# Spreading the steps of the later modulation vectors over other stages, and reading the input back in sixteen pieces

## The chip, the cores and the metric

The kernel runs on one core of one Trainium2 chip. The metric is the device time of one execution in microseconds (us); the median of the runs counts.

## The reference, cut to what matters

One transformer block over 256 tokens of width 2048, with a context of 256 more tokens. A conditioning vector gives six modulation vectors; the block mixes a two-way recurrence and a windowed attention, and ends in a convolutional feed-forward part.

```python
mod_x = adaln(c, w_ada[l], b_ada[l])          # silu(c) @ w_ada + b_ada: 6 vectors of 2048
px = split_projection(modulate(x, norm1_g[l], mod_x[:, 0], mod_x[:, 1]) @ w_in[l])
rec_x, _, _ = hgrn2_bidirectional(px[0], px[1], px[2], px[3], px[4], lb, hgrn_norm_g[l], s_f, s_b)
att_x = windowed_attention(qx, kx, vx, kc, vc, attn_sink[l])
mix_x = gated_merge(rec_x, att_x, px[8], px[9], w_rec_proj[l], w_att_proj[l], w_out[l])
x_mid = x + mod_x[:, 2][:, None, :] * mix_x
ffn_x = conv_ffn(modulate(x_mid, norm2_g[l], mod_x[:, 3], mod_x[:, 4]), w_up[l], conv_w[l], conv_b[l], w_down[l])
new_x = x_mid + mod_x[:, 5][:, None, :] * ffn_x
```

The vectors 0 and 1 are needed at once. The vectors 2, 4, 3 and 5 (in the order of their use) are the "later modulation vectors" of this document: 2 is first needed in the output projection, 4 there too, 3 behind it, 5 in the down projection.

## The kernel before

**Weights.** All weights lie in one stream in HBM in the order of their use, in halves of 512 KB (eight tiles of 128x128, float32). `Stream.load` (L104 to L112) takes one half: SyncE issues the DMA into `raw` (four buffers), ScalarE rounds it into `whi` (L109), VectorE forms the rest `wlo` (L110); both have three buffers. TensorE multiplies with both parts. A load is put 60 instructions (`LEAD`) ahead of its use in the order by which the compiler places instructions. SyncE, VectorE and TensorE then each run their own list in that order: an instruction that waits holds all behind it on its engine.

**Stages**, in order of time in the trace (us): start and first projections to 149; the heads, 149 to 490; the attention's query projection to 548; the output gate of the recurrence with attention beside it to 615; the gates of the merge to 704, with the rest of the attention in it; the merge (sixteen column tiles, in eight pairs) to 889; the output projection (eight pairs, `mid_evac` behind each tile) to 985; up and down projections to the end.

**One head** `h` has two directions `d`. For each, `tform_all` (48 matmuls, two weight halves) makes the gate, and `hgrn_a` turns it into decays on ScalarE and VectorE. `hgrn_q` (L491) then prepares operands for `hgrn_b` (L506), the first small matmuls of the head, which TensorE has in its list in the next head, one `tform_all` later. Heads 4 and 6 are preceded by a `natural` projection, a long stretch of matmuls with little VectorE work.

**Steps.** `ada_steps` (L320) makes the later vectors: four vectors in two parts are eight blocks. A block is sixteen steps, each of which loads 512 KB of `w_ada` through GpSimd's DMA queue into `araw` (two buffers, L330) and adds it, scaled, into `acc` on VectorE (L333, L335); then two empty steps; then one that transposes `acc` on TensorE (L343) and reduces it (L344). `ada(n)` (L355) takes the next n of the 152 steps where it is called, 60 instructions (`LAG`) behind that place and behind the last `wlo` written so far. What the stages take is thus written out by hand as numbers in the calls of `ada`.

**The input.** `xm` (L761) takes the input again, to be added to the output projection's result. It has the place in memory (`qo`) of the recurrence's output, which is free once `y_rec` (L721, called in the gates) has read it. Two loads of 1 MB (L763), issued by SyncE; in the list of SyncE they stand where that place comes free.

Of the kernel before, what the change touches and what calls it, by code (L numbers as in the profile page):

```python
# [7 lines left out]
F32 = mybir.dt.float32  # L8
# [6 lines left out]
P = 128  # L15
T = 256
D = 2048
KT = D // P
# [32 lines left out]
def block_kernel(ctx, tc, xct, prm, cst, ada2, wst, out):  # L51
    nc = tc.nc
    V, S, PE = nc.vector, nc.scalar, nc.tensor

    cons = ctx.enter_context(tc.tile_pool(name="cons", bufs=1))
    big = ctx.enter_context(tc.tile_pool(name="big", bufs=1))
# [6 lines left out]
    def bank(pool=None):  # L63
        pool = pool or mm
        return pool.tile([P, 512], F32, name="bank" + ("m" if pool is mm else "s"))
# [20 lines left out]
    def par(n):  # L86
        o, w = POFF[n]
        return prm_t[:, o:o + w]
# [9 lines left out]
    class Stream:  # L98
# [20 lines left out]
        def next(self, n=1):  # L119
            if self.pos == 8:  # L120
                self.load()
            sl = slice(self.pos * P, (self.pos + n) * P)
            self.pos += n
            return self.hi[:, sl], self.lo[:, sl]
# [187 lines left out]
    qo = big.tile([P, 2, H, T], F32, name="qo", tag="qo")  # L312
# [42 lines left out]
    def ada(n=1):  # L355
        with tc.high_priority(offset=-LAG), tc.issue_after(st.last.ins):
            for _ in range(n):
                next(ada_it, None)
# [33 lines left out]
    def tform_all(o):  # L392
        for k in range(KT):
            mm3(o, *st.next(), hi_all(k), lo_all(k), k == 0, k == KT - 1)
            if k % 8 == 7:
                tick()

    def fold(dst, o):
        S.copy(dst, o[:, 0:T])
        V.tensor_tensor(dst, o[:, T:], dst, op=ALU.add)  # L400

    def natural(banks, tts):
        for i in range(8):
            ws = [st.next(4) for _ in range(2)]
            for b, tt in zip(banks, tts):
                for k2 in range(2):
                    kt = 2 * i + k2
                    mm3(b, *tok(kt, tt), *ws[k2], kt == 0, kt == KT - 1)
            tick()
# [81 lines left out]
    def hgrn_q(h):  # L491
        S.activation(QI, B_[:, :, 0:T], AF.Exp)
        for d in range(2):
            V.tensor_copy(dec[:, d, :], QI[:, d].rearrange("p (c t) -> p c t", t=CH)[:, :, LAST[d]])
        V.tensor_tensor(QI, QI, qo[:, 0, h, None, :].broadcast_to([P, 2, T]), op=ALU.mult)
        for d in range(2):
            c1, c2 = d, 1 - d
            q2 = QI[:, d].rearrange("p (a c t) -> p a c t", a=2, c=2)[:, :, c2, :]
            V.tensor_copy(QC[:, d], q2)
            V.tensor_tensor(q2, q2, dec4[:, d, :, c1, None].broadcast_to([P, 2, CH]), op=ALU.mult)  # L500
            kf = K_[:, d, d * P:d * P + P]
            V.tensor_scalar(K2[:, d, CH * c1:CH * c1 + CH], kf[:, CH * c1:CH * c1 + CH], dec4[:, d, d, c2:c2 + 1], None, op0=ALU.mult)
            V.tensor_copy(K2[:, d, CH * c2:CH * c2 + CH], kf[:, CH * c2:CH * c2 + CH])
            V.tensor_tensor(decb[:, d:d + 1], dec4[:, d, d, 0:1], dec4[:, d, d, 1:2], op=ALU.mult)
# [82 lines left out]
    def kv_evac(banks):  # L587
        kns = {}

        def norm(tt):  # L590
            S.copy(va[:, tt, :], banks[tt][:, 256:512])
            kn = scr.tile([P, 512], F32, name="t")
            headnorm(kn[:, 0:256], banks[tt][:, 0:256], 2, par("kg"))
            if tt < 2:
                rope(kn[:, 0:256], kn[:, 0:256], tt, 2, kn[:, 256:512])
            kns[tt] = kn

        def trans(tt):
            kn = kns.pop(tt)
            tp = bank(ms)  # L600
            for kv in range(2):
                PE.transpose(tp[:, kv * P:kv * P + P], kn[:, kv * P:kv * P + P], ident)
            S.copy(kT[:, :, tt * P:tt * P + P], tp[:, 0:256].rearrange("p (k e) -> p k e", k=2))

        def nxt(tt):
            trans(tt)
            if tt < 3:
                norm(tt + 1)
        norm(0)
        tasks.extend([lambda tt=tt: nxt(tt) for tt in range(4)])  # L610

    for h in range(H):
        if h == 4:
            bs = [bank() for _ in range(4)]
            natural(bs, range(4))
            ada(4)
            for tt in range(4):
                S.copy(vn[:, tt, 512:1024], bs[tt])
        if h == 6:
            bs = [bank() for _ in range(4)]  # L620
            natural(bs, range(4))
            ada(4)
            kv_evac(bs)
        for d in range(2):
            if 2 * h + d < 3:
                o = early_f[2 * h + d]
            else:
                o = bank()
                tform_all(o)
            hgrn_a(h, d, o)  # L630
            ada(0 if h > 5 else 2 if h else 1)
        hgrn_q(h)
        tasks += [lambda h=h: hgrn_e(h - 1), lambda h=h: hgrn_b(h), lambda h=h: hgrn_c(h), lambda h=h: hgrn_d(h)]
        ada(1)
        if h == 0:
            q_heads(4)
# [12 lines left out]
    for g in range(2):  # L649
        if g:  # L650
            bs = [bank() for _ in range(2)]
        natural(bs, range(2))
        ada(1)
        if not g:
            assert not tasks
            gr = big.tile([P, KT, T], F32, name="gr", tag="v")
            aq = gr[:, 0:H, :].rearrange("p (a c) t -> p a (c t)", a=2)
            PB = gr[:, H:, :].rearrange("p (h k) t -> p h (k t)", h=4)
        for tt in range(2):
            qn = aq[:, tt, g * 512:g * 512 + 512]  # L660
            headnorm(qn, bs[tt], 4, par("qg"))
            tmp = scr.tile([P, 512], F32, name="t")
            rope(qn, qn, tt, 4, tmp)

            def trans(g=g, tt=tt, qn=qn):
                tp = bank(ms)
                for i in range(4):
                    PE.transpose(tp[:, i * P:i * P + P], qn[:, i * P:i * P + P], ident)
                hs, ts = slice(4 * g, 4 * g + 4), slice(tt * P, tt * P + P)
                split(qTh[:, hs, ts], qTl[:, hs, ts], tp.rearrange("p (h e) -> p h e", h=4))  # L670
            tasks.append(trans)
# [44 lines left out]
    for h in range(0, H, 2):  # L716
        for i, o in enumerate(duo((xx, xx))):
            fold(qo[:, 0, h + i, :], o)
        ada(2)

    def y_rec(p):  # L721
        hs = slice(2 * p, 2 * p + 2)
# [4 lines left out]
    for j in range(0, KT, 2):  # L727
        for i, o in enumerate(duo((xx, xx))):
            fold(gr[:, j + i, :], o)
        if YR <= j < YR + 4:  # L730
            assert not tasks
            y_rec(j - YR)
            y_rec(j - YR + 1)
            ada(2)
        else:
            ada(2 + 2 * (j >= 8))
    for j in range(0, KT, 4):
        S.activation(gr[:, j:j + 4, :], gr[:, j:j + 4, :], AF.Sigmoid)

    assert not tasks, len(tasks)  # L740
    yb = big.tile([P, KT, 2, T], F32R, name="yb", tag="b")
    for j in range(0, KT, 2):
        gas = []
        for o in duo((xx, xx)):
            ga = scr.tile([P, 512], F32, name="t")
            fold(ga[:, 0:T], o)
            sig = S.activation(ga[:, 0:T], ga[:, 0:T], AF.Sigmoid)
            gas.append(ga)
        for i, ga in enumerate(gas):
            orec, oatt = duo((yre, yat), 8)  # L750
            fold(ga[:, T:], orec)
            V.tensor_tensor(gr[:, j + i, :], gr[:, j + i, :], ga[:, T:], op=ALU.mult)
            fold(ga[:, T:], oatt)
            V.tensor_tensor(ga[:, 0:T], ga[:, 0:T], ga[:, T:], op=ALU.mult)
            V.tensor_tensor(ga[:, 0:T], ga[:, 0:T], gr[:, j + i, :], op=ALU.add)
            split(yb[:, j + i, 1, :], yb[:, j + i, 0, :], ga[:, 0:T])
            ada(0 if j + i == 15 else 3 if i else 2)

    with tc.issue_after(sig.ins):
        S.preload_act_table_set("natural_log_exp_and_others")  # L760
    xm = big.tile([P, KT, T], F32, name="xm", tag="qo")  # L761
    for i in range(2):
        nc.sync.dma_start(xm[:, 8 * i:8 * i + 8, :], xct[:, 8 * i:8 * i + 8, 0:T])  # L763
    gate1, sc2, sh2, gate2 = [modv[:, i, :] for i in range(4)]
    ssa = scr.tile([P, 512], F32, name="rs", bufs=1)
    xa = big.tile([P, KT, T], F32, name="xa", tag="v")
# [19 lines left out]
    for j in range(0, KT, 2):  # L786
        for i, o in enumerate(duo((yb, yb))):
            with tc.high_priority(offset=RUSH if j == KT - 2 else 0):
                mid_evac(j + i, o)
        if 2 <= j < 8:  # L790
            ada(2 if j < 6 else 1)
        if j == 10:
            split(pre[:, 0, :, T:], pre[:, 1, :, T:], sh2[:, :, None].broadcast_to([P, KT, 2]))

# [229 lines left out]
```

## Time and profile before

| | us |
|---|---|
| median of three runs (1720.06 to 1724.96) | 1720.73 |
| the profiled execution's own time | 1723.61 |
| its span, first to last instruction | 1721.8 |
| TensorE busy in the span | 1692.8 |
| VectorE busy | 1203.1 |
| ScalarE busy | 837.4 |

The difference between own time and span lies before the first and behind the last instruction. TensorE's share (98%) is an average: where it is idle has to be read stage by stage, and the same holds for VectorE's 70%.

### The profile page before, as it was taken

The numbers are of one execution on the slowest core, as the hardware profiler recorded it, in microseconds if no ns is written. First come the engines' busy times: TensorE is split into PE (matmuls) and PEld (weight loads), VectorE is DVE, ScalarE is ACT, GpSimd is POOL, SyncE is SP. The second block draws the span as 40 slices with busy tenths as digits, with TensorE's granted clock in tenths as the row PEclk, the third lists the DMA queues.
The fourth block names the chain that finished last, engine by engine and source line by source line (L and its number), as shares of the span: only waits on it lengthen the run. The fifth ranks groups of instructions, "written<-read, shape, count | busy, mean of one in ns | idle before, by whom it ended". The sixth has DMA issues, their size and how long they took to land.

```text
span 1721.8 us, 24746 instructions
## 1 busy us (share of the span) xinstructions
PE 1692.8 (98%) x9438; PEld 1430.6 (83%) x9438; DVE 1203.1 (70%) x1890; ACT 837.4 (49%) x1278; POOL 69.0 (4%) x132
## 2 busy tenths in 40 slices
PE   6999999999999999999999999999999999999999
PEld 2668888888888887888888998888888888888887
DVE  4438876565669887788878797777766655666565
ACT  4237443342555665455554565555555434554332
POOL 0000100100000001010100000000000000000000
PEclk9999999999999999999999999999999999999999
DMA  9986724624345658787877567777655555555564
GB/s 375 379 331 223 258 98 158 196 80 153 111 135 192 212 185 292 265 288 246 310 242 231 190 223 259 231 249 252 232 183 185 194 184 195 184 194 186 190 201 148
DMA packets 104008, 371.84 MB, mean 216 GB/s; under 512 B 11344, under 2 KB 13776, under 8 KB 103888
## 3 DMA queue, kind: packets, MB, share of 16 engines
q1 hardware_dynamic: 85456, 303.14, 51.1%
q0 software_dynamic: 18432, 67.12, 12.1%
q8 instruction: 74, 1.21, 0.3%
q14 instruction: 46, 0.38, 0.1%
HBM read 368.11 MB, written 2.10 MB: 215 GB/s over the span
## 4 chain that ended last, share of the span: by engine, by line
PE 85%; DMA 6%; DVE 5%; issue 3%; ACT 1%; SPq 0%; POOL 0%; DVEq 0%; POOLq 0%; ACTq 0%
PE bankm L68 77%; PE banks L68 5%; DMA araw<-in_ada_dram 5%; DVE wlo L110 1%; DVE acc L335 1%; DMA ringq<-in_wst_dram 1%; ACT whi L109 1%; DVE xraw L230 0%; PE banks L343 0%; PE banks L524 0%; PE banks L532 0%; PE banks L698 0%; SPq L116 0%; ACT t L220 0%; PE banks L533 0%
## 5 line engine op out<-in xcount | busy, mean ns | idle before, releaser
L68 PE MATMUL bankm<-hl,whi 128*128 128x512 f32 (+1 forms) x3392 | 1055.1, 392 | 0.7 <-DVE t L400 0.7
L110 DVE TENSOR_TENSOR wlo<-raw,whi 128x1024 fp32r<-128x1024 f32 x498 | 606.0, 1219 | 301.4 <-ACT whi L109 299.9
L109 ACT CAST whi<-raw 128x1024 fp32r<-128x1024 f32 x498 | 520.4, 1046 | 555.6 <-PE bankm L68 481.2
L68 PEld LDWEIGHTS bankm<-hl,wlo 128*128 128x128 f32 x3104 | 582.8, 188 | 140.7 <-DVE wlo L110 9.5
L68 PE MATMUL bankm<-hl,wlo 128*128 128x256 f32 (+2 forms) x3104 | 665.1, 287 | 6.6 <-DVE wlo L110 6.4
L68 PEld LDWEIGHTS bankm<-hl,whi 128*128 128x128 f32 x3392 | 534.7, 189 | 21.1 <-DVE t L400 1.0
L335 DVE SCALAR_TENSOR_TENSOR acc<-araw,csil,acc 128x1024 f32<-128x1024 f32 x120 | 153.7, 1281 | 36.4 <-DMA araw<-in_ada_dram 35.7
L68 PE MATMUL bankm<-whi,hl 128*128 128x512 f32 x512 | 166.6, 398 | 3.3 <-ACT hl L206 2.6
L68 PEld LDWEIGHTS bankm<-whi,hl 128*128 128x128 f32 x512 | 96.7, 189 | 25.4 <-ACT hl L206 4.4
L330 POOL DMA_DIRECT2D araw<-in_ada_dram x128 | 68.8, 537 | 1153.8 <-DVE acc L335 664.5
L68 PE MATMUL bankm<-wlo,hl 128*128 128x512 f32 x256 | 100.5, 393 | 0.0
L68 PE MATMUL bankm<-yb,whi 128*128 128x512 f32 x256 | 80.8, 397 | 0.0
L68 PE MATMUL bankm<-g,whi 128*128 128x512 f32 x256 | 80.4, 395 | 0.0
L68 PEld LDWEIGHTS bankm<-g,wlo 128*128 128x128 f32 x256 | 48.1, 188 | 11.4
L68 PEld LDWEIGHTS bankm<-yb,wlo 128*128 128x128 f32 x256 | 48.1, 188 | 11.3
L68 PEld LDWEIGHTS bankm<-wlo,hl 128*128 128x128 f32 x256 | 48.5, 190 | 9.6
L849 DVE SCALAR_TENSOR_TENSOR xm<-bankm,modv,xm 128x256 f32<-128x256 f32 x96 | 42.2, 480 | 18.4 <-PE bankm L68 18.3
L831 ACT ACTIVATE fs<-fs,prm 128x256 f32<-128x256 f32 x44 | 26.5, 602 | 55.9 <-DVE fs L400 55.9
L68 PE MATMUL bankm<-yb,wlo 128*128 128x256 f32 x256 | 50.6, 279 | 0.0
L68 PE MATMUL bankm<-g,wlo 128*128 128x256 f32 x256 | 50.3, 278 | 0.0
L195 DVE TENSOR_REDUCE tn<-banks 128x8 f32<-128x32 f32 x8 | 1.5, 191 | 65.9 <-ACT whi L109 51.4
L832 DVE SCALAR_TENSOR_TENSOR fs<-fs,prm,fs 128x255 f32<-128x255 f32 x44 | 21.3, 484 | 26.7 <-ACT fs L831 26.7
(214 smaller groups left out, 1242.1 us busy)
## 6 DMA issues: line engine op xcount, KB each, us to landing
raw<-in_wst_dram SPq DMA_DIRECT2D x490, 512.0 KB, 4.0
araw<-in_ada_dram POOLq DMA_DIRECT2D x128, 512.0 KB, 4.7
ringv<-in_wst_dram SPq DMA_DIRECT2D x24, 512.0 KB, 8.7
ringq<-in_wst_dram SPq DMA_DIRECT2D x20, 512.0 KB, 9.6
araw<-in_wst_dram SPq DMA_DIRECT2D x10, 512.0 KB, 8.8
xraw<-in_xct_dram SPq DMA_DIRECT2D x8, 512.0 KB, 10.2
raw<-in_wst_dram SPq DMA_DIRECT2D x8, 384.0 KB, 8.4
ringkT<-in_wst_dram SPq DMA_DIRECT2D x5, 512.0 KB, 10.2
```

What stands on the lines that cost most here:

```text
L68: return PE.matmul(o, l, r, start=start, stop=stop, skip_group_check=True)
L109: S.copy(hi, raw)
L110: self.last = V.tensor_tensor(lo, raw, hi.bitcast(F32), op=ALU.subtract)
L195: V.tensor_reduce(m8, aps.rearrange("p (q g c) -> p q c g", q=4, g=4)[:, :, 0:2, :], axis=AX.X, op=ALU.add)
L330: nc.gpsimd.dma_start(raw, ada2[idx])
L335: V.scalar_tensor_tensor(acc, raw, csil[:, kt, 0:1], acc, op0=ALU.mult, op1=ALU.add)
L831: S.activation(t, s, AF.Identity, bias=cb[:, f:f + 1], scale=cw[:, f, 1:2])
L832: V.scalar_tensor_tensor(t[:, 1:T], s[:, 0:T - 1], cw[:, f, 0:1], t[:, 1:T], op0=ALU.mult, op1=ALU.add)
L849: V.scalar_tensor_tensor(xm[:, j, :], o[:, T * i:T * i + T], gate2[:, j:j + 1], xm[:, j, :], op0=ALU.mult, op1=ALU.add)
```

## The change

The number of steps that each stage takes is set anew; the steps themselves and their order stay. By the calls, the stages took and take:

| stage | steps before | steps after |
|---|---|---|
| heads | 46 | 68 |
| query projection | 2 | 4 |
| output gate | 8 | 12 |
| gates | 20 | 16 |
| merge | 37 | 16 |
| output projection | 5 | 8 |
| up projection | 34 | 28 |

The two loads of `xm` behind the merge become sixteen of 128 KB in it, one for each column tile. Each is held back by a copy of one column into the place that it will write (VectorE, 128x1), which itself reads the tile's `ga` after its second fold.

```diff
         if h == 4:
             natural(bs, range(4))
-            ada(4)
+            ada(6)
...
         if h == 6:
             natural(bs, range(4))
-            ada(4)
+            ada(6)
...
             hgrn_a(h, d, o)
-            ada(0 if h > 5 else 2 if h else 1)
+            ada(2 if h > 5 else 3 if h else 1)
...
         natural(bs, range(2))
-        ada(1)
+        ada(2)
...
     for h in range(0, H, 2):
         for i, o in enumerate(duo((xx, xx))):
             fold(qo[:, 0, h + i, :], o)
-        ada(2)
+        ada(3)
...
         else:
-            ada(2 + 2 * (j >= 8))
+            ada(2)
...
+    xm = big.tile([P, KT, T], F32, name="xm", tag="qo")
     for j in range(0, KT, 2):
...
             fold(ga[:, T:], oatt)
+
+            V.tensor_copy(xm[:, j + i, 0:1], ga[:, T:T + 1])
+            nc.sync.dma_start(xm[:, j + i, :], xct[:, j + i, 0:T])
             V.tensor_tensor(ga[:, 0:T], ga[:, 0:T], ga[:, T:], op=ALU.mult)
...
-            ada(0 if j + i == 15 else 3 if i else 2)
+            ada(1)
...
-    xm = big.tile([P, KT, T], F32, name="xm", tag="qo")
-    for i in range(2):
-        nc.sync.dma_start(xm[:, 8 * i:8 * i + 8, :], xct[:, 8 * i:8 * i + 8, 0:T])
...
-        if 2 <= j < 8:
-            ada(2 if j < 6 else 1)
+        if 2 <= j < 10:
+            ada(2)
```

## Rows read from the trace of the kernel before

**Rows 1.** The page, busy time, share of the span and instructions of each engine.

```profile
PE 1692.8 (98%) x9438; PEld 1430.6 (83%) x9438; DVE 1203.1 (70%) x1890; ACT 837.4 (49%) x1278; POOL 69.0 (4%) x132
```

**Rows 2.** By stage: stretch; length; PE, PEld, DVE, ACT, POOL busy; clock; DMA; GB/s.

```profile
149.00:490.00 341.00, 336.63 (x1723) 283.58 (x1722) 233.98 (x449) 152.46 (x266) 23.19 (x42) 0.99 0.47 156
...
548.00:615.00 67.00, 67.00 (x385) 58.17 (x384) 55.02 (x100) 46.96 (x79) 3.18 (x6) 1.00 0.59 193
615.00:704.00 89.00, 84.95 (x484) 72.73 (x483) 70.03 (x102) 48.71 (x75) 8.48 (x16) 1.00 0.77 266
704.00:889.00 185.00, 182.59 (x1052) 158.50 (x1051) 154.71 (x212) 93.52 (x145) 16.96 (x32) 1.00 0.80 274
889.00:985.00 96.00, 96.00 (x573) 84.58 (x571) 77.05 (x129) 47.63 (x72) 2.12 (x4) 1.00 0.63 205
```

**Rows 3.** Waits of TensorE from 140 us on: waiter, releaser, total, times, longest.

```profile
PE bankm L68 <- DVE wlo L110: 6.4, 5, 3.1
```

**Rows 4.** Timeline, late gates, one engine after another: start, length, operation [idle before].

```profile
679.70 0.50 PE L68 MATMUL bankm<-hl,wlo 128*128 128x256 f32 x2 [0.76 <-DVE wlo L110]
688.65 0.50 PE L68 MATMUL bankm<-hl,wlo 128*128 128x256 f32 x2 [3.10 <-DVE wlo L110]
...
686.18 1.28 DVE L335 SCALAR_TENSOR_TENSOR acc<-araw,csil,acc 128x1024 f32<-128x1024 f32 x1 [3.47 <-DMA araw<-in_ada_dram]
...
665.84 0.39 SPq L763 DMA_DIRECT2D xm<-in_xct_dram  x1
...
671.80 0.68 SPq L763 DMA_DIRECT2D xm<-in_xct_dram  x1
```

**Rows 5.** Late gates: busy time (as rows 2), and a DMA issue (KB each, us to landing).

```profile
682.00:693.00 11.00, 7.91 (x46) 6.58 (x45) 7.53 (x9) 4.00 (x4) 1.59 (x3) 1.00 0.85 327
...
xm<-in_xct_dram SPq DMA_DIRECT2D x2, 1024.0 KB, 10.4
```

**Rows 6.** Instructions on `araw`: durations in ns, least, median, most.

```profile
L335 DVE SCALAR_TENSOR_TENSOR acc<-araw,csil,acc x120: 1267/1281/1289, 157.3 to 1232.1; 128x1024 f32<-128x1024 f32 x120
...
L329 DVE COPY araw<-prm x2: 144/146/147, 148.4 to 148.4; 128x1 f32<-128x1 f32 x2
```

**Rows 7.** Head 1: timeline of ScalarE, VectorE, TensorE; busy time (as rows 2) behind it.

```profile
210.33 0.63 ACT L466 ACTIVATE hb<-hb 128x512 f32<-128x512 f32 x1
...
216.15 0.54 DVE L467 TENSOR_SCALAR hb<-hb,lb_t 128x512 f32<-128x512 f32 x1
...
221.67 1.18 PE L68 MATMUL banks<-hb 128*64 128x64 f32 x8 [1.78 <-DVE hb L499]
...
223.00:225.00 2.00, 1.98 (x8) 1.75 (x9) 2.00 (x9) 1.34 (x3) 0.00 (x0) 0.50 0.00 0
```

**Rows 8.** Head 3, second direction: timeline of VectorE and TensorE.

```profile
277.15 1.29 DVE L335 SCALAR_TENSOR_TENSOR acc<-araw,csil,acc 128x1024 f32<-128x1024 f32 x1 [1.17 <-DMA araw<-in_ada_dram]
...
283.77 0.19 DVE L503 COPY hb<-hb 128x64 f32<-128x64 f32 x1
...
284.17 3.35 PE L68 MATMUL banks<-hb 128*128 128x128 f32 x24
```

**Rows 9.** Heads 4 and 5: `hgrn_a` of their second directions on VectorE; busy time (as rows 2).

```profile
348.72 0.55 DVE L467 TENSOR_SCALAR hb<-hb,lb_t 128x512 f32<-128x512 f32 x1 [0.69 <-ACT hb L466]
...
376.43 0.55 DVE L467 TENSOR_SCALAR hb<-hb,lb_t 128x512 f32<-128x512 f32 x1 [0.82 <-ACT hb L466]
...
338.90:386.00 47.10, 47.10 (x237) 39.58 (x237) 33.85 (x84) 24.33 (x45) 0.74 (x1) 1.00 0.26 87
```

**Rows 10.** Output projection, busy time (as rows 2) of a stretch with steps and one without.

```profile
923.00:934.00 11.00, 11.00 (x65) 9.62 (x64) 10.81 (x18) 4.91 (x9) 1.06 (x2) 1.00 0.73 230
...
956.00:967.00 11.00, 11.00 (x65) 9.63 (x64) 8.45 (x15) 5.67 (x9) 0.00 (x0) 1.00 0.59 194
```

**Rows 11.** The end: a wait of SyncE's queue, and small DMA issues (as rows 3, 5).

```profile
SPq L862 <- DVE xm L849: 11.0, 2, 8.0
...
out_dram<-xm SPq DMA_DIRECT2D x2, 128.0 KB, 1.8
```

## Prediction

> **What bounds the kernel now.** Read the busy times first: TensorE works 1692.8 of 1721.8 us [rows 1]. The 29 us that are left are all that a change of this kind can give, and most of them lie in the start, which it doesn't touch. So the next view is the busy time by stage, where the reader looks for stages in which TensorE's column is shorter than the stage: 4.37 us are missing in the heads, none in the output gate, 4.05 in the gates, 2.41 in the merge, none in the output projection [rows 2]. The waits say who ended the pauses: from 140 us on, five waits for `wlo`, 6.4 us, are the largest entry [rows 3]. By the timeline four of these five lie in gates and merge, and the two largest, 0.76 and 3.10 us, are in the late gates [rows 4].
>
> There two things meet. The two 1 MB loads of `xm` are issued at 665.84 and 671.80 us [rows 4], as soon as their place is free and not where the code has them; they take 10.4 us to land, and even behind them the DMA share is 0.85 at 327 GB/s [rows 5], where gates and merge together have 0.77 and 0.80 [rows 2]. In the same pairs the kernel takes four steps instead of two, so VectorE comes to additions whose data is still under way: one waits 3.47 us, and the `wlo` behind it in VectorE's list lets TensorE wait 3.10 us [rows 4]. In the merge VectorE is busy 154.71 of 185 us [rows 2] and the pauses are of the same kind, only shorter.
>
> The heads' missing time is another matter. [...]
>
> **The change part by part.** *Steps leave gates and merge.* An addition takes 1.28 us on VectorE [rows 6]. Counting which of the moved steps are additions (a block has sixteen, then two empty steps, then the transposition), the gates lose three of sixteen, the merge nineteen of 32. The merge's VectorE falls from 154.7 by 19 x 1.28 = 24.3 us to 130.4 of 182.6 us. In the gates the groups of four are gone. I take all 4.05 + 2.41 = 6.46 us as gained: in the output gate and the output projection VectorE is as busy (82% and 80%) and TensorE has no pause [rows 2]. The lower bound of the gain is what the two largest waits name, 3.86 us [rows 4].
>
> *The sixteen loads.* They move the same 2 MB in the merge, over 185 us instead of some 16. The nearest rows for one are the 128 KB stores at the end, 1.8 us to landing, and the 1 MB loads, 10.4 us [rows 5, 11]; 16 x 1.8 = 29 us of flight in 185 us, beside other transfers: nothing on the path. Each tile's load is wanted by `mid_evac` in the next stage, so it is early by a stage. The sixteen copies cost VectorE 16 x 0.145 = 2.3 us [rows 6], covered by the 24.3 us that leave; without that cover they would cost at most that. The new wait is SyncE's: it waits for the copy, and behind it stand the weight loads. The end of the kernel shows such a wait, 8.0 us long, with weight loads behind it [rows 11], and no `wlo` wait falls there. I take 0; the other end is a rival below.
>
> [...]
>
> *Steps enter the heads.* Nineteen more additions, 24.3 us, and one more transposition, whose matmuls are only moved. Over the stage that fits: VectorE has 234 of 341 us [rows 2]. Head by head it doesn't quite. A head lasts 376.43 - 348.72 = 27.7 us; without additions VectorE is busy 33.85 of 47.1 us, so 19.9 us per head [rows 9]; seven additions make 28.9 us, 1.2 more than there is. Heads 2 to 5 are of that kind; what is over can fall into the two `natural` stretches behind heads 3 and 5. What counts is VectorE's work from the end of `tform_all` to `hgrn_b`. In head 3 an addition already lies in it, with 1.17 us of waiting for its data; VectorE ends at 283.96, TensorE comes at 284.17 without a pause [rows 8]. So 0.2 us of slack are left there with one addition of 2.5 us, some 2.7 without. Seven steps in a head put one or two there. The bounds: below, the 5.35 us of head 1 are given back (-5.35); above, two more heads like head 1 (+10.7). I take half of the 1.2 us in each of four heads, **+2.0 us**, nearer to head 3, which is as dense (two steps 3.4 us apart) and pauses nowhere.
>
> *Steps enter output gate and output projection.* Three more additions and a transposition make 55.0 + 3.8 + 1.5 of 67 us, 90%; I take 0. In the output projection a pair without steps uses 8.45 of 11 us of VectorE; two additions make 11.0 of 11 in four pairs running. One stretch with 10.81 is there, with no pause [rows 10]. Bounds 0 and four pauses like 0.76 [rows 4], 3.0; I take **+0.5**. The up projection loses six steps and had no pause: 0.
>
> The sum: -6.46 + 2.0 + 0.5 = **-4.0 us**. The profiled execution took 1723.61 us, 2.9 above the median of 1720.73; it becomes 1719.6, and the median 1716.7.
>
> **The rivals.** *The heads take everything without a pause* (head 3 speaks for it, the 28.9 of 27.7 us against): -6.46, 1714.3. *The pause of head 1 goes as well*: -11.8, 1708.9; the steps of heads 0 and 1 change little (block one has only sixteen additions, and all came before head 1's `hgrn_a`), so it is unlikely.
>
> *Slower: heads that pause as head 1 does.* The mechanism: VectorE's list is fixed, an addition that waits for its DMA holds `hgrn_a` and `hgrn_q`, TensorE reaches `hgrn_b` first, pauses, and loses half its clock. Price 5.35 us per head. From 6.46 / 5.35 = 1.2 heads on it eats the gain: two heads give 1725.0, three 1730.3. For it: head 1, and a slack of 0.2 us. Against: in the heads the DMA share is 0.47, in the merge 0.80 [rows 2], so data lands sooner.
>
> [...]
>
> *Slower: SyncE's queue.* If a wait for the copy holds the weight loads longer than the buffers last, each tile may pause. At 1 us for each of sixteen tiles, it is +16: 1730.3 together with the gain. It decides from waits as long as the 8.0 us of the end [rows 11], if they come with all buffers empty.
>
> *The stalls only move* (to output gate and output projection): 1720.7.
>
> **How the numbers follow.** Forecast 1716.7: 0.45, its own range 1713.5 to 1720. Heads without pause 0.20; head 1 cured too 0.08; heads with clock loss 0.14, half of it two heads, half three or more; the queue 0.05; moved only 0.08. A measurement of this kernel tells about 0.3% from no change, 5.2 us: faster means under 1715.6, slower over 1725.9. Faster: 0.20 + 0.08 + 0.09 of the forecast's own = 0.37. Slower: 0.07 + 0.05 = 0.12. The rest, 0.51, is the same. The range reaches from 1708, for the cured head 1, to 1727, for two heads with clock loss; it leaves out three such heads and the queue, 0.12.
>
> **What would show it.** Right: `xm` issues spread through the merge, no 1 MB issue near 666 us, gates and merge with TensorE busy throughout, VectorE at some 73% of the merge; in the heads waits of the small matmuls for `hb` of some 2 us in all beside head 1's. Wrong: waits for `wlo` still in gates or merge (then it was not the burst); clock under 1.00 in heads 2 to 7; SyncE waits on the copy with `whi` late behind it.

## The result, and the profile after

| | before | after |
|---|---|---|
| median (20 runs each), us | 1723.3 | 1728.93 |
| lowest to highest, us | 1718.79 to 1731.86 | 1721.5 to 1738.97 |
| profiled execution, own time, us | 1723.61 | 1725.86 |
| its span, us, and its mean granted clock | 1721.8, 0.997 | 1723.8, 0.994 |

The ratio of after to before is 1.0033, its 95% interval 1.0018 to 1.0047: slower by some 0.3%, where 0.2% faster was forecast. The median of before lies 2.6 us above that of the three runs of the prediction.

First the busy time by stage (stretch; length; PE, PEld, DVE, ACT, POOL busy; clock; DMA share; GB/s), to be laid beside [rows 2].

```profile
149.00:490.00 341.00, 330.86 (x1677) 278.71 (x1676) 243.47 (x445) 144.64 (x252) 32.58 (x60) 0.98 0.55 180
...
548.00:615.00 67.00, 66.15 (x383) 57.15 (x382) 62.65 (x110) 45.44 (x75) 5.61 (x11) 1.00 0.66 213
615.00:704.00 89.00, 88.90 (x513) 77.23 (x512) 64.32 (x104) 52.94 (x86) 3.36 (x7) 1.00 0.59 196
704.00:889.00 185.00, 185.00 (x1066) 161.48 (x1065) 141.76 (x205) 93.90 (x146) 9.49 (x18) 1.00 0.74 246
889.00:985.00 96.00, 96.00 (x564) 84.25 (x563) 81.53 (x134) 48.83 (x73) 4.22 (x8) 1.00 0.69 239
```

The stretches are the same times in both traces, while the changed kernel lags by 10.5 us at the last head and 2.9 us at the output projection (below), so its rows hold slightly earlier work. Gates and merge now miss 0.10 us of TensorE together, where they missed 4.05 and 2.41. The heads miss 10.14 us instead of 4.37, at a clock of 0.98 instead of 0.99. The waits of TensorE from 140 us on (waiter, releaser, total, times, longest) say who ended the pauses:

```profile
PE banks L68 <- DVE hb L499: 8.6, 6, 3.1
PE banks L68 <- DVE hb L536: 1.0, 1, 1.0
...
PE bankm L68 <- DVE wlo L110: 0.8, 1, 0.8
```

The `wlo` waits of [rows 3] are all but gone, and in their place stands the first operand of `hgrn_b` (L499), which is the pause that head 1 had in [rows 7]. TensorE's timeline has the larger ones in heads 4 and 6 (start, length, operation, in brackets the idle time before it and what ended it):

```profile
220.81 1.18 PE L68 MATMUL banks<-hb 128*64 128x64 f32 x8 [1.52 <-DVE hb L499]
...
283.67 2.87 PE L68 MATMUL banks<-hb 128*64 128x64 f32 x20 [0.97 <-DVE hb L499]
...
359.83 4.76 PE L68 MATMUL banks<-hb 128*64 128x64 f32 x20 [2.30 <-DVE hb L499]
...
470.56 3.42 PE L68 MATMUL banks<-hb 128*64 128x64 f32 x20 [3.07 <-DVE hb L499]
```

How the wait comes about is read from VectorE's timeline in head 4, second direction:

```profile
350.06 1.28 DVE L335 SCALAR_TENSOR_TENSOR acc<-araw,csil,acc 128x1024 f32<-128x1024 f32 x1 [2.12 <-DMA araw<-in_ada_dram]
351.26 0.54 DVE L467 TENSOR_SCALAR hb<-hb,lb_t 128x512 f32<-128x512 f32 x1
...
352.74 1.28 DVE L335 SCALAR_TENSOR_TENSOR acc<-araw,csil,acc 128x1024 f32<-128x1024 f32 x1 [0.47 <-DMA araw<-in_ada_dram]
...
356.65 1.28 DVE L335 SCALAR_TENSOR_TENSOR acc<-araw,csil,acc 128x1024 f32<-128x1024 f32 x1
...
359.55 0.23 DVE L499 COPY hb<-hb 128x128 f32<-128x128 f32 x1
```

One addition stands ahead of `hgrn_a` and two between it and `hgrn_b`'s operand. Two of the three find their data not yet landed, and VectorE stands still for 2.12 + 0.47 = 2.59 us, which is a little more than TensorE's pause of 2.30. The additions themselves take 3.8 us there, so that this row alone leaves open which of the two is too much; the experiments below separate them. Head 6 has the same picture: 1.34 + 1.55 = 2.89 us of waiting for data in two additions, 3.07 us of pause:

```profile
461.09 1.28 DVE L335 SCALAR_TENSOR_TENSOR acc<-araw,csil,acc 128x1024 f32<-128x1024 f32 x1 [1.34 <-DMA araw<-in_ada_dram]
...
464.27 1.29 DVE L335 SCALAR_TENSOR_TENSOR acc<-araw,csil,acc 128x1024 f32<-128x1024 f32 x1 [1.55 <-DMA araw<-in_ada_dram]
```

Behind these two pauses the granted clock is down to 0.50. Busy time in short stretches around head 4's pause, and behind head 6's (columns as above, the clock third from the end):

```profile
358.00:360.00 2.00, 0.17 (x2) 0.17 (x2) 2.00 (x8) 1.71 (x3) 0.53 (x1) 0.99 0.36 49
360.00:362.00 2.00, 2.00 (x10) 1.65 (x10) 2.00 (x7) 0.00 (x0) 0.00 (x0) 0.50 0.56 221
...
366.00:368.00 2.00, 2.00 (x9) 1.59 (x8) 1.31 (x3) 1.01 (x2) 0.00 (x0) 0.80 0.22 47
...
474.00:476.00 2.00, 2.00 (x8) 1.90 (x9) 1.90 (x2) 0.99 (x3) 0.00 (x0) 0.50 0.88 297
```

From 360 to some 367 us TensorE has 0.50 (0.52 in the mean of these 7 us), which costs 3.4 us.

**Where the time went.** The same instruction in both traces gives the lead or lag at its place. The `hgrn_a` of the second direction of heads 4 and 5 stood at 348.72 and 376.43 [rows 9]; after, at 351.26 (above) and at

```profile
383.07 0.54 DVE L467 TENSOR_SCALAR hb<-hb,lb_t 128x512 f32<-128x512 f32 x1
```

so the lag is 2.5 us and then 6.6; the 28 us between them hold head 4's pause and its half clock. Read on like this, the changed kernel is 0.9 us ahead at the first head (start differs by that), 10.5 behind at the last one (491.20 against 480.69), 2.9 behind at the first `mid_evac`, and 2.0 at the end. The heads cost 11.4 us, and the way to the output projection gives back 7.6. The 11.4 are made up so: the pauses from 149 to 500 us sum to 10.58 us against 4.24, so 6.3 more; half clock behind heads 1, 4 and 6 (granted in the mean: 0.81 from 221 to 230 us, 0.52 from 360 to 367, 0.82 from 470 to 474 and 0.50 to 476) costs 1.7 + 3.4 + 1.7 = 6.8 us against 3.4 before (0.52 from 223 to 230), so 3.4 more; the remaining 1.7 us were not read by themselves, but are about the size of the third transposition (eight matmuls of 0.27 us), which now lies in the heads and no longer behind them.

**One profile is not the median.** Of the 20 executions after, the fastest (1721.5) had a mean granted clock of 0.997, the slowest (1738.97) 0.990. The span times what is missing of the clock, 5.2 and 17.4 us, makes up 12.2 of the 17.5 us between them. The median of that product is 11.2 us over the 20 runs after, and 5.2 us over 29 runs of before, taken on another chip for the experiments. This difference of 6.0 us is as large as that of the medians, 5.6. The clock is on record to three decimals, so each product is good to 0.9 us only. By this estimate the pauses gained in gates and merge and those lost in the heads came out even, and the lost clock makes the kernel slower.

### The profile page after: what moved, and what is told of

It is laid out like the page before. It is cut to its first block, busy times and chain, and to the rows that moved or that the text cites. A ratio compares the mean times of both kernels' runs of the same rounds, so it can differ in the third digit from the quotient of the medians.

```text
span 1723.8 us, 24762 instructions
## 1 busy us (share of the span) xinstructions
PE 1695.1 (98%) x9438; PEld 1433.9 (83%) x9438; DVE 1204.6 (70%) x1906; ACT 835.4 (48%) x1278; POOL 68.9 (4%) x132
## 4 chain that ended last, share of the span: by engine, by line
PE 75%; issue 11%; DMA 7%; DVE 5%; ACT 1%; SPq 0%; POOL 0%; POOLq 0%; DVEq 0%; ACTq 0%
PE bankm L68 70%; DMA araw<-in_ada_dram 6%; PE banks L68 4%; DVE acc L335 1%; DVE wlo L110 1%; DMA ringq<-in_wst_dram 1%; DVE xraw L230 0%; PE banks L343 0%; PE banks L698 0%; DVE hb L473 0%; DVE hb L474 0%; DVE hb L489 0%; PE banks L524 0%; SPq L116 0%; ACT t L220 0%
## 5 line engine op out<-in xcount | busy, mean ns | idle before, releaser
L68 PEld LDWEIGHTS bankm<-yb,wlo 128*128 128x128 f32 x256 | 48.1, 188 | 11.4
L68 PEld LDWEIGHTS bankm<-g,wlo 128*128 128x128 f32 x256 | 48.1, 188 | 11.4
L68 PE MATMUL banks<-hb 128*128 128x128 f32 (+2 forms) x256 | 39.3, 285 | 9.8 <-DVE hb L499 8.6
L68 PEld LDWEIGHTS banks<-hb 128*128 128x128 f32 (+1 forms) x256 | 33.6, 187 | 16.1 <-DVE hb L499 9.7
```

The source lines that it names most:

```text
L68: return PE.matmul(o, l, r, start=start, stop=stop, skip_group_check=True)
```

## The experiments

Three theories stood at the start. Theory A: gates and merge gain what was forecast, and the heads' added steps take more than that, by pauses and clock. Theory B: the sixteen loads with their copies cost something. Theory C: VectorE is short of time wherever the steps are put. Each ratio is to the kernel before on the same chip: its median was 1723.81 us for the first four kernels below (29 runs), 1724.91 for the next four (29 runs) and 1724.68 for the last (14 runs).

**The sixteen loads alone**, on the kernel before, its steps untouched:

```diff
+    xm = big.tile([P, KT, T], F32, name="xm", tag="qo")
     for j in range(0, KT, 2):
...
+            V.tensor_copy(xm[:, j + i, 0:1], ga[:, T:T + 1])
+            nc.sync.dma_start(xm[:, j + i, :], xct[:, j + i, 0:T])
...
-    xm = big.tile([P, KT, T], F32, name="xm", tag="qo")
-    for i in range(2):
-        nc.sync.dma_start(xm[:, 8 * i:8 * i + 8, :], xct[:, 8 * i:8 * i + 8, 0:T])
```

> The kernel before with the sixteen loads of xm alone; all steps stay where they were. Theory A (the steps in the heads made the kernel slower, the loads are innocent): the two pauses of the late gates (0.76 and 3.10 us) go, heads as before, so 1 to 5 us faster than before (ratio 0.997 to 1.000). Theory B (the loads hold SyncE's queue or VectorE in the merge): slower than before by some 5 us (ratio about 1.003), with raw loads late in the merge.

Measured: 1722.01 us (12 runs), ratio 0.9982 (0.9969 to 0.9994). In time the loads cost nothing and seem to bring a little. In the late gates one pause is left where [rows 4] have 0.76 and 3.10 us; the merge on the other hand misses 5.42 us instead of 2.41, in a profiled execution that was the slowest of the twelve (1726.51 us). Timeline of TensorE and busy time by stage of this kernel:

```profile
686.48 0.50 PE L68 MATMUL bankm<-hl,wlo 128*128 128x256 f32 x2 [1.41 <-DVE wlo L110]
```

```profile
704.00:889.00 185.00, 179.58 (x1021) 155.38 (x1020) 152.37 (x221) 90.90 (x142) 16.89 (x32) 0.99 0.82 279
```

**The steps alone**, the two 1 MB loads as before:

```diff
-            V.tensor_copy(xm[:, j + i, 0:1], ga[:, T:T + 1])
-            nc.sync.dma_start(xm[:, j + i, :], xct[:, j + i, 0:T])
...
+    for i in range(2):
+        nc.sync.dma_start(xm[:, 8 * i:8 * i + 8, :], xct[:, 8 * i:8 * i + 8, 0:T])
```

> The changed kernel with the two 1 MB loads of xm as before. Theory A: pauses of the heads as in the changed kernel (some 7 us of waiting on hb in heads 3 to 7 and half clock behind the long ones), and perhaps a pause in the late gates comes back: ratio 1.003 to 1.006 to before. Theory B: without the loads no slower than before, ratio 0.997 to 1.000.

Measured: 1727.05 us (12 runs), ratio 1.002 (1.0003 to 1.0036), so the slowdown comes with the steps. Its heads pause like those of after; but the expected pause in the late gates did not come back. Waits of TensorE, and the gates' busy time:

```profile
PE banks L68 <- DVE hb L499: 11.2, 5, 4.4
```

```profile
615.00:704.00 89.00, 88.91 (x507) 77.04 (x505) 65.49 (x102) 52.76 (x84) 4.22 (x8) 1.00 0.68 225
```

The burst of 2 MB makes no pause in the gates once the groups of four steps are gone.

**The heads' steps put back**: the heads as before, 46 steps, two steps per tile in the merge, the rest as after.

```diff
-            ada(6)
+            ada(4)
...
-            ada(2 if h > 5 else 3 if h else 1)
+            ada(0 if h > 5 else 2 if h else 1)
...
-            ada(1)
+            ada(2)
```

> The changed kernel with the heads' 46 steps of before; the 22 steps go back into the merge mostly (two per tile there, regularly, instead of one). Theory A: the pauses of heads 3 to 6 go, gates and merge stay almost without pauses, so 3 to 7 us faster than before (ratio 0.996 to 0.998). Theory B: as slow as the changed kernel (1.003). Theory C (VectorE is simply short of time, wherever the steps are): new pauses of 2 to 5 us in the merge, ratio about 1.000.

Measured: 1727.46 us (12 runs), ratio 1.0022 (1.0003 to 1.004). Theory A missed. The heads are again as before (336.20 of 341 us), but the merge, at two steps for every tile, misses 7.51 us, three times what it missed before. TensorE waits there for `fold` (L400), with which VectorE takes a tile's results out of a bank of TensorE. Busy time of the merge, and the waits:

```profile
704.00:889.00 185.00, 177.49 (x998) 153.32 (x998) 147.55 (x213) 87.37 (x137) 15.32 (x29) 0.98 0.77 261
```

```profile
PE bankm L68 <- DVE t L400: 7.7, 5, 3.5
```

VectorE's timeline shows what holds the `fold` at the second largest of these pauses: two additions ahead of it wait 1.70 and 2.58 us for their data (the second addition, the `fold`, and TensorE behind it).

```profile
727.09 1.28 DVE L335 SCALAR_TENSOR_TENSOR acc<-araw,csil,acc 128x1024 f32<-128x1024 f32 x1 [2.58 <-DMA araw<-in_ada_dram]
...
729.42 0.42 DVE L400 TENSOR_TENSOR t<-bankm,t 128x256 f32<-128x256 f32 x1
...
729.89 0.50 PE L68 MATMUL bankm<-hl,whi 128*128 128x512 f32 x1 [1.89 <-DVE t L400]
```

So the heads are not a place that is worse than others in itself: C has something for it, and whether VectorE is short of time or of data was the next question.

**The heads' steps all behind the first direction**, as many per head as after, so that none stands between the second `tform_all` and `hgrn_b` by the calls:

```diff
-            ada(2 if h > 5 else 3 if h else 1)
+            ada((0 if d else 5 if h > 5 else 7) if h else 1)
...
-        ada(1)
+        ada(0 if h else 1)
```

> The changed kernel with the same number of steps in each head, but all of them called behind the head's first direction, none behind the second one and hgrn_q. If their place decides (steps that stand in VectorE's list between the second direction's tform_all and hgrn_b): pauses on hb in heads 3 to 6 shrink from 6.6 us to under 2, ratio to before 0.996 to 0.999. If their number decides (seven steps of 1.28 us in a head of 27.7 us with 19.9 us of other work): pauses as in the changed kernel, ratio about 1.003.

Measured: 1733.47 us (6 runs), ratio 1.0051 (1.0033 to 1.0069), the slowest of all and slower than either expectation. TensorE has 326.71 of 341 us in the heads at a clock of 0.95, and its largest pause is longer than any of after:

```profile
479.00 0.69 PE L524 MATMUL banks<-cst,hb 128*128 128x128 f32 x2 [4.09 <-DVE hb L502]
```

The additions asked for in one place don't stay there: the last of them finds its data late, behind the second `hgrn_a`, by VectorE's timeline of the same head, and what `hgrn_b` needs stands behind it.

```profile
467.71 0.54 DVE L467 TENSOR_SCALAR hb<-hb,lb_t 128x512 f32<-128x512 f32 x1
...
471.34 1.29 DVE L335 SCALAR_TENSOR_TENSOR acc<-araw,csil,acc 128x1024 f32<-128x1024 f32 x1 [3.09 <-DMA araw<-in_ada_dram]
```

**The heads' loads left out.** The two blocks whose additions fall between some 240 and 420 us (loads 16 to 47) add a tile that is already there; 32 loads of 512 KB are not made, VectorE's work stays.

```diff
-                    raw = strm.tile([P, 1024], F32, name="araw", bufs=2)
...
-                    nc.gpsimd.dma_start(raw, ada2[idx])
+                    if not 16 <= idx < 48:
+                        raw = strm.tile([P, 1024], F32, name="araw", bufs=2)
...
+                        nc.gpsimd.dma_start(raw, ada2[idx])
```

> The changed kernel, but the additions of blocks 2 and 3 (the ones that run in heads 2 to 6) read one tile that is there already instead of loading their own: 32 loads of 512 KB are left out, the additions stay. If waiting for data is what delays hgrn_q (2.0 to 2.9 us of waits in the chains of heads 4 and 6): the pauses on hb behind head 1 fall from 7.1 us to under 2, ratio to before 0.994 to 0.998. If VectorE's time itself is what is short (seven additions of 1.28 us): pauses of 4 to 7 us stay, ratio 1.000 to 1.003.

**The heads' additions made short.** The other way round: the same blocks keep their loads, and the additions take 128 of 1024 columns.

```diff
+                        w = 128 if 16 < idx <= 48 else 1024
-                        V.scalar_tensor_tensor(acc, raw, csil[:, kt, 0:1], acc, op0=ALU.mult, op1=ALU.add)
+                        V.scalar_tensor_tensor(acc[:, 0:w], raw[:, 0:w], csil[:, kt, 0:1], acc[:, 0:w], op0=ALU.mult, op1=ALU.add)
```

> The changed kernel with all its loads, but in blocks 2 and 3 an addition takes 128 of the 1024 columns (about 0.3 instead of 1.28 us); the rest is left out. If VectorE's time is short: pauses on hb behind head 1 fall under 2 us and the ratio to before to 0.994 to 0.998. If it is the waiting for data: the waits stay or grow, since each addition now comes sooner, pauses of 3 to 7 us, ratio 1.000 to 1.003.

Measured: without loads 1722.2 us (10 runs), ratio 0.9984 (0.9967 to 1.0001); with short additions 1728.21 us (10 runs), ratio 1.0017 (1.0001 to 1.0033). The same stretch, 230 to 455 us, in four kernels: before, after, without loads, with short additions.

```profile
230.00:455.00 225.00, 225.00 (x1125) 189.02 (x1125) 136.88 (x263) 88.23 (x156) 12.62 (x23) 1.00 0.41 134
```

```profile
230.00:455.00 225.00, 221.45 (x1097) 185.96 (x1096) 144.83 (x273) 83.47 (x149) 18.89 (x35) 0.98 0.49 157
```

```profile
230.00:455.00 225.00, 224.98 (x1125) 188.94 (x1124) 148.54 (x278) 86.71 (x155) 2.64 (x5) 1.00 0.27 90
```

```profile
230.00:455.00 225.00, 221.58 (x1097) 186.05 (x1097) 118.43 (x273) 84.28 (x150) 18.66 (x35) 0.98 0.47 157
```

VectorE's column decides nothing: the kernel in which it is busiest, 148.54 us, keeps TensorE busy throughout, and the one in which it has 30 us less misses 3.42 us and has 0.98 of the clock. What goes with the pauses is the data. In the kernel with short additions VectorE waits for it for 28.9 us in this stretch (waits of VectorE), and the largest pause of TensorE comes behind such waits:

```profile
DVE acc L336 <- DMA araw<-in_ada_dram: 28.9, 14, 6.0
```

```profile
287.76 3.66 PE L68 MATMUL banks<-hb 128*64 128x64 f32 x20 [3.40 <-DVE hb L500]
```

In after it is 9.1 us, without the loads 2.4 (in the next block, whose loads stayed), and before 7.8, but there nine waits of at most 1.4 us, none long enough to bring `hgrn_b` late. Head 6, whose loads stayed in the kernel without loads, still pauses there, for 2.99 us, and so does head 1 (3.97 us). So the pauses behind head 1 fell to 3 us, not under 2, and the ratio came to 0.9984, just short of what was expected. Leaving loads out also takes traffic away (a DMA share of 0.27 instead of 0.49), so this run alone doesn't tell late data from busy DMA.

Head 1 does. Up to it VectorE's list is the same in after, in the run of the steps alone and in these two kernels, and none of its own loads is left out or its additions shortened. Only the waits for data differ from execution to execution. Here are one of these waits and TensorE's pause behind it, in after (whose pause of 1.52 us, at 220.81, stands above) and without the loads:

```profile
211.46 1.29 DVE L335 SCALAR_TENSOR_TENSOR acc<-araw,csil,acc 128x1024 f32<-128x1024 f32 x1 [1.52 <-DMA araw<-in_ada_dram]
```

```profile
214.77 1.28 DVE L335 SCALAR_TENSOR_TENSOR acc<-araw,csil,acc 128x1024 f32<-128x1024 f32 x1 [3.85 <-DMA araw<-in_ada_dram]
...
223.83 4.44 PE L68 MATMUL banks<-hb 128*64 128x64 f32 x20 [3.97 <-DVE hb L499]
```

Over the last five additions ahead of head 1's `hgrn_b` the waits sum to 3.85, 4.33, 5.87 and 7.10 us in the steps alone, after, the short additions and without the loads, and the pauses are 0.76, 1.52, 3.55 and 3.97 us: the longer the data is late, the longer TensorE waits, with the same work. It also says how far one trace goes: the same list gives pauses that are 3 us apart. More room for the data (a third buffer of `araw`) wasn't tried.

**The heads' steps put back, with the two loads**: the kernel with the heads' 46 steps and two steps per tile in the merge, and the two 1 MB loads instead of the sixteen.

```diff
-            V.tensor_copy(xm[:, j + i, 0:1], ga[:, T:T + 1])
-            nc.sync.dma_start(xm[:, j + i, :], xct[:, j + i, 0:T])
...
+    for i in range(2):
+        nc.sync.dma_start(xm[:, 8 * i:8 * i + 8, :], xct[:, 8 * i:8 * i + 8, 0:T])
```

> Heads as before, two steps per tile in the merge (as heads_back), and the two 1 MB loads of xm instead of the sixteen. If the sixteen copies and loads are what hurt beside steps in the merge (heads_back paused 7.5 us there, before 2.4 with more steps): merge pauses under 3 us, ratio to before 0.997 to 0.999. If it is the steps in output gate and merge themselves: as heads_back, 1.000 to 1.003.

Measured: 1724.44 us (12 runs), ratio 1.001 (0.9996 to 1.0024). The merge still misses 5.66 us (179.34 of 185), so the copies in it are not what makes a merge of two steps per tile worse than before's two and three. Again it goes with the data: in the merge VectorE's additions wait 19.6 us for it here and 19.0 us in the kernel with the sixteen loads, against 11.6 us before and 2.2 us after. In the kernel with the sixteen loads four of them follow each other so: two from 741.94 us on, one at 748.23 and one at 751.98, and the last two wait 0.68 and 2.47 us. That `araw` has only two buffers may be why, but that is not shown.

**Steps inside the natural projections.** These have little of VectorE's work, and no `hgrn_b` waits on it. Two steps behind each of the first seven weight halves of the two late `natural` stretches, one per direction in heads 0 to 5 and one in each of heads 6 and 7, 24 in the merge:

```diff
-    def natural(banks, tts):
+    def natural(banks, tts, steps=0):
...
             tick()
+            if i < 7:
+                ada(steps)
...
-            natural(bs, range(4))
-            ada(6)
+            natural(bs, range(4), 2)
...
-            ada(2 if h > 5 else 3 if h else 1)
+            ada(0 if h > 5 else 1)
         hgrn_q(h)
...
-        ada(1)
+        ada(1 if h > 5 or h == 0 else 0)
...
-            ada(1)
+            ada(2 if i else 1)
```

> The changed kernel with the heads' steps put where VectorE has time: two after each of seven weight halves inside the natural projections of heads 4 and 6, one per direction elsewhere (51 instead of 68 in the heads), and three instead of two per pair of tiles in the merge. If the heads' chains from tform_all to hgrn_b are the cause: no pause on hb over 0.7 us behind head 1, merge pauses under 3 us, 3 to 7 us faster than before, ratio 0.996 to 0.998. If steps cost the same wherever they are: ratio 1.001 to 1.003.

Measured: 1715.64 us (6 runs, 1714.01 to 1717.67), ratio 0.9951 (0.9935 to 0.9967): faster than both kernels, and by more than was expected. Heads and merge by busy time, and the longest pause, in TensorE's timeline:

```profile
149.00:490.00 341.00, 336.17 (x1741) 283.50 (x1740) 239.95 (x453) 152.40 (x267) 24.06 (x46) 1.00 0.49 165
...
704.00:889.00 185.00, 185.00 (x1066) 161.45 (x1065) 149.68 (x222) 95.53 (x148) 11.10 (x21) 1.00 0.79 265
```

```profile
428.86 0.41 PE L604 MATMUL banks<-cst,t 128*128 128x128 f32 x2 [2.50 <-DVE t L577]
```

51 steps lie in the heads, more than before, and no `hgrn_b` is late for its first operands (a wait of 0.65 us inside the last one is there before, too). Head 1's pause is gone, and the granted clock is 1.00 in every stage of the profiled execution; the product of span and missing clock is 2.6 us in the median. Yet VectorE waits longer for its data than in either kernel: 31.4 us in the heads (149 to 490 us), against 19.1 us in after and 14.6 before. The longest wait lies in the first late `natural` stretch, and TensorE is busy throughout there (all 58 us from 279 to 337). Waits of VectorE, and that wait:

```profile
DVE acc L335 <- DMA araw<-in_ada_dram: 31.4, 20, 4.0
```

```profile
303.78 2.60 DVE L335 SCALAR_TENSOR_TENSOR acc<-araw,csil,acc 128x1024 f32<-128x1024 f32 x2 [3.95 <-DMA araw<-in_ada_dram]
```

So it is not how long VectorE waits in all that counts, but whether the wait stands between the end of a `tform_all` and `hgrn_b`. The edit does two things at once, fewer steps in these chains and more in the `natural` stretches, and doesn't tell what each gives.

**The same with the two 1 MB loads**, issued at 664.7 and 667.6 us; the edit is that of the run of steps alone.

> The kernel of the run naturals with the two 1 MB loads of xm instead of the sixteen. If the burst of these loads is what made the late gates pause, and not the groups of four steps: pauses on wlo of 2 to 4 us come back in the late gates, and it is 2 to 4 us slower than naturals (ratio to before 0.997 to 0.998). If the groups of four were the cause: no pause there, as fast as naturals (0.995), and the sixteen loads do nothing of their own.

Measured: 1717.24 us (9 runs), ratio 0.9964 (0.9952 to 0.9976). The two intervals overlap, and the pauses of 2 to 4 us that the burst was to bring are not there:

```profile
615.00:704.00 89.00, 89.00 (x515) 77.66 (x515) 66.28 (x99) 51.16 (x79) 5.80 (x11) 1.00 0.70 237
```

## Why the prediction was wrong

**Gates and merge: right.** 6.46 us were taken, 6.36 came, VectorE in the merge is at 77% (73% forecast). The cause given was half right. The burst alone makes no pause on `wlo` there (three runs), the groups of four alone leave one of 1.41 us (sixteen loads alone); the 3.86 us of before came with both. The prediction called 0.76 and 3.10 us the two largest of the five waits; by TensorE's timeline before, 0.76 is the smallest, and the merge has 0.86 and 0.88, so the 3.86 us are those of the late gates and no more. And that the merge gained hangs on how its steps are spread: at one step per tile, or three per pair, it has no pause; at two per tile it misses 7.51 and 5.66 us, more than the 2.41 of before.

**The sixteen loads and SyncE's queue: right.** In the merge SyncE waits for the copies thirteen times, 0.5 us at the longest (put down to L759, which stands right behind the copy in VectorE's list), and a load lands in 4.1 us (waits of SyncE; DMA issues: times, KB each, us to landing):

```profile
SPq L758 <- DVE t L759: 6.6, 13, 0.5
```

```profile
xm<-in_xct_dram SPq DMA_DIRECT2D x16, 128.0 KB, 4.1
```

That is longer than the 1.8 us of the nearest row [rows 11], and off the path. The 8.0 us wait of the end told nothing about this queue. With two loads of 1 MB in their place the time is the same within its interval (0.9951 and 0.9964, the kernels with steps in the `natural` stretches). The landings, sixteen of 4.1 us against two of 10.4 us [rows 5], decide nothing in the time.

**Output gate, output projection: small misses that cancel.** The output gate, taken at 0, misses 0.85 us; the output projection, taken at 0.5, misses nothing.

**The heads: this step failed.** +2.0 us stood in the sum, half of the 1.2 us by which a head's VectorE sum exceeds a head, four times (which would be 2.4), and nothing for the clock. Measured: 6.3 us of pauses and 3.4 us of clock in the profiled execution, 9.7 in all, near the step's upper bound of 10.7. The size came from the wrong quantity. Busy time summed over a head does not pause TensorE, as the kernel without the loads shows, with the same additions and no pause in heads 3 to 5, and the kernel with short additions from the other side. What counts is the standstill that an addition brings into VectorE's fixed list when its data has not landed, if it stands between `tform_all` and `hgrn_b`; the four traces of head 1 and the kernel with steps in the `natural` stretches show it. The prediction had that mechanism, in head 3, with 1.17 us of waiting and 0.2 us of slack left [rows 8], and then read this row for its good end: no pause. The row said that a second wait like it would be 1 us too many. A step more per direction makes these waits 2.6 to 2.9 us, and the pauses follow them.

**The rival that came** is that of heads that pause as head 1 does. The price of 5.35 us a head is what head 1 of before shows: pauses of 1.78 us [rows 7] and 0.17 us, and a granted clock that falls to 0.50 [rows 7] and has a mean of 0.80 and then 0.52 over 5 us each, 5 x 0.20 + 5 x 0.48 = 3.4 us (TensorE's timeline and busy time before):

```profile
223.02 2.98 PE L68 MATMUL banks<-hb 128*128 128x128 f32 x12 [0.17 <-DVE hb L485]
```

```profile
220.00:225.00 5.00, 3.15 (x16) 2.65 (x17) 4.68 (x19) 4.31 (x10) 0.00 (x0) 0.80 0.02 8
225.00:230.00 5.00, 5.00 (x19) 4.20 (x18) 3.19 (x5) 1.82 (x4) 0.00 (x0) 0.52 0.60 202
```

The two larger pauses after cost 2.30 + 3.4 and 3.07 + 1.7 us, 10.5 together, against 2 x 5.35 by that price. What was said against it, that the heads' DMA share is only 0.47 and data lands sooner, failed: the share rose to no more than 0.55, and data was late in bursts that a share over 341 us doesn't show. With two such heads its median was 1725.0 and, 2.9 us above it as in the forecast, its profiled execution 1727.9; measured were 1728.93 and 1725.86. So it has the mechanism and the direction, and the time only roughly. The range reached to 1727 and missed the median by 1.9 us. In part that is the base: before itself came 2.6 us higher in 20 runs than in the three, and the change of +5.6 us by itself would have ended at 1726.4 from the three runs' median, just inside. The direction was wrong on either base. And the clock takes different amounts in different executions, 5 to 17 us: the price of 3.4 us for one pause, read off one execution, was taken for fixed.

**What would show it.** Of the signs named for a wrong forecast, clock under 1.00 in heads 2 to 7 came, and this one alone. Of those for a right one, the one on the heads failed: beside head 1 the waits of the small matmuls for `hb` (L499) came to 7.1 us, not some 2.

## What to carry to other kernels

Before work is moved onto an engine with a fixed list, add up not its busy time but the waits for data that it brings along, between the input and the output for which another engine waits: a load that lands late there stops everything behind it (in head 4 here, 2.59 us of such waits and 2.30 us of pause). The sum of the waits over a stage says as little as that of the busy time: the fastest kernel here has 31.4 us of them in the heads, the changed one 19.1. Put such work into long stretches in which nobody waits for that engine soon, as in the natural projections here, and let a stage that has no pauses keep its slack. Where the time of a kernel varies with the granted clock (here a mean of 0.990 to 0.997 over 20 executions of one kernel), price a pause by many executions, not by the one that was profiled.

## What the hardware showed that was not expected

In these traces the pauses of TensorE do not cost the clock by their length alone. Ahead of `hgrn_b`, 1.78 us [rows 7], 2.30 and 3.07 us were followed by 0.50, and 0.97 us was not (1.00 from 284 to 290 us, after); in the merge of the kernel with the heads' steps put back, 1.89 us was followed by 0.66 in the mean of the next 5 us. But 3.10 us in the gates before [rows 5] and 2.50 us in front of the attention's transpositions of the natural-projection kernel had 1.00 on either side:

```profile
427.00:430.00 3.00, 1.14 (x6) 1.03 (x7) 3.00 (x5) 0.72 (x3) 0.00 (x0) 1.00 0.73 205
430.00:433.00 3.00, 3.00 (x15) 2.44 (x14) 2.93 (x10) 1.88 (x5) 0.53 (x1) 1.00 0.77 254
```

One and the same program had a mean granted clock of 0.990 in one execution and 0.997 in another (after). No run here shows why one pause lost the clock and another did not.
